# The order of wide and narrow products in a feed-forward layer: alternating, or in runs of one width

## The chip, the core and the metric

The kernel runs on one core of a Trainium2 chip. The metric is the device time of one execution in microseconds, the median of several. TensorE (PE in the profile) multiplies, VectorE (DVE) and ScalarE (ACT) do the elementwise work, GpSimd (POOL) a few small things, and SyncE (SP) issues the loads of the weights.

## What is computed

A decoder trunk of four layers over 256 tokens of width 1024, in float32. Each layer normalises its input, mixes tokens (differential attention, block-sparse attention, sliding-window attention, and differential attention again), adds the result to the residual stream, and then does the same with a feed-forward block; a last normalisation follows. The change is in the feed-forward block alone:

```python
def sqrelu_mlp(h, w_up, w_down):          # w_up 1024 x 4096, w_down 4096 x 1024
    a = jnp.maximum(h @ w_up, 0)
    return (a * a) @ w_down

for i in range(DEPTH):
    ...
    h = h + y                             # y: the token mixer
    h = h + sqrelu_mlp(rms_norm(h, mlp_norm_g[i]), mlp_w_up[i], mlp_w_down[i])
return rms_norm(h, final_norm_g)
```

## The kernel before

Float32 products are made out of products of a faster type, fp32r. Each operand x is split into a high part, x rounded to fp32r, and a low part, the rest. A product is then high times high, plus high times low, plus low times high. Weights arrive in 185 pieces of 128 x 2048 numbers (class `Piece`): SP loads a piece into `raw`, ACT writes the high part `whi`, DVE writes the low part `wlo`, each in two halves of 1024 columns. Four `raw` and three `whi`/`wlo` buffers go round. The activations are kept the same way: for the up projection in `n.both` (tiles hg0 to hg3, `n.lo` is the task that finishes the low part), for the down projection in the tiles uu, listed in `us`. In both, the high and the low part of a block of 128 rows lie side by side, 256 tokens each, so that one matmul can stream both: 512 columns.

That is what `block_step` uses. With a block of 128 x 128 weights stationary, its first matmul streams high and low activations past the high weights, 512 columns, into the whole of a PSUM bank; its second streams the high activations past the low weights, 256 columns, into the first half of the same bank. Eight such steps make a block of 128 rows of the up projection, 32 a block of the down projection. The two halves of the bank are added afterwards (`joined`, tiles cross and relu).

- `up_proj`: 16 groups g of one piece each; a group makes two blocks b of 128 rows (two banks of one PSUM pair, `p_up`), each summed over 8 blocks k of the input. In group 0 the list is sorted by k, since the inputs arrive one after another.
- `down_proj` (layers 0 to 2): 8 blocks d of the output in `p_down`, two pieces h each, 16 steps k per piece.
- `down_out` (layer 3): here the activations are stationary and the weights stream, so that the output comes out with tokens on partitions. There are two halves c of 512 output columns, for each 8 pieces q with 4 steps k, and two token blocks t. Each step is three matmuls (`mm3`) into `p_last`. In the second half, token block 1 is computed as two blocks of 256 columns, and in the last piece one of them is finished before the other. Behind it stand `ended` (DVE adds the residual into `res`, ACT squares it for the norm, DVE multiplies by the gain into `last`) and `send` (a mean on DVE, a power on POOL, and the scaling and the output transfers on ACT with its queue and on DVE with SP's).

The order of all instructions is set by a planner (class `Plan`) at build time: each task has a cost in microseconds and the tasks that it waits for, the planner simulates the engines with those costs, and the instructions are issued in the order of its start times. Main products (`product`) are chained: each waits for the one written before it, so their order among themselves is that of the code. The costs given to `product` decide only what the planner believes of the time. Nothing of the costs is executed. Every instruction has line 191 of the helper class `Ordered` in the profile, so groups are told apart by tile names.

Of the kernel before, what the change touches and what calls it, by code (L numbers as in the profile page):

```python
# [18 lines left out]
P = 128  # L19
D = 1024  # L20
S = 256
NT = S // P
# [175 lines left out]
def trunk(ctx: ExitStack, tc: tile.TileContext, xT, gains, lams, swa_row, fng, weights, out):  # L198
# [8 lines left out]
    def bank(name, i=0):  # L207
        j = plan.now.got["wk"][i] if plan.now else 0
        return ps.tile([P, 512], F32, tag=f"wk{j}", name=name, bufs=1)
# [8 lines left out]
    def r3(n):  # L218
        return lambda t: t.rearrange("p (a b) -> p a b", a=n)
# [23 lines left out]
    def pe(cost, do, after=(), rank=1, **kw):  # L243
        return add("PE", cost, do, after, lag=0.3, rank=rank, **kw)
# [3 lines left out]
    def product(cost, do, after, take=None):  # L248

        main[0] = t = pe(cost, do, [*after, main[0]], 2, take=take)  # L250
        main[1] += cost
        t.done = main[1]
        return t

    def matmul(o, lhsT, rhs, start, stop):
        T.matmul(o, lhsT, rhs, start=start, stop=stop, skip_group_check=True)
# [4 lines left out]
    def mm3(o, lh, ll, rh, rl, start, stop):  # L261
        matmul(o, lh, rh, start, False)
        matmul(o, lh, rl, False, False)
        matmul(o, ll, rh, False, stop)
# [47 lines left out]
    def piece(**kw):  # L312
        pieces.append(Piece(len(pieces), **kw))
        return pieces[-1]

    def release(x):
        give("w", [main[0]], x.hi[0])
# [222 lines left out]


    PRODUCTS = ((0, 0), (1, 0), (0, 1))

    def proj(n, width, **kw):

# [3 lines left out]
        for x in range(count):  # L549
            w = piece(**kw)  # L550
            ks = range(per * x, per * x + per)
            steps = [(t, k, a, b) for k in ks for a, b in PRODUCTS for t in range(NT)]
            for at, (t, k, a, b) in enumerate(steps):
# [431 lines left out]

    def block_step(p, hi, lo, x, start, stop):
        matmul(r3(2)(p), hi, x, start, False)
        matmul(p[:, :S], lo, x[:, 0], False, stop)  # L990

    def joined(o, p, after):

# [41 lines left out]
    def up_proj(n, then):  # L1035

        us = []
        for g in range(16):
            w = piece()
            st = {}  # L1040
            order = [(b, k) for b in range(2) for k in range(8)]
            if g == 0:
                order.sort(key=lambda x: x[1])
            for at, (b, k) in enumerate(order):

                def do(b=b, k=k, w=w, st=st):
                    if not st:
                        st["p"] = two_banks("p_up")
                    c = slice(P * b, P * b + P)
                    block_step(st["p"][:, b], w.at(0, 8, k)[:, c], w.at(1, 8, k)[:, c], n.both[k // 2][:, k % 2],  # L1050
                               k == 0, k == 7)

                t = product(0.347, do, [n.lo[k], w.ready(1, 8, k)], {"acc": 1} if at == 0 else None)
                begin = t if at == 0 else begin
            release(w)

            def sum_to(st=st):
                st["t"] = sb.tile([P, 512], F32, tag="relu", name="relu")
                return r3(2)(st["t"])

            a = joined(sum_to, lambda st=st: st["p"], [t])
            give("acc", [a], begin)

            def squared(st=st):
                st["u"] = sb.tile([P, 512], F32, tag="u", name="u")
                V.scalar_tensor_tensor(st["u"], st["t"], 0.0, st["t"], op0=OP.max, op1=OP.mult)

            def high(st=st, g=g):
                st["both"] = room(g, [P, 2, 2, S], "uu", F32R)
                A.activation(st["both"][:, :, 0], r3(2)(st["u"]), AF.Copy)  # L1070

            def low(st=st):
                V.tensor_tensor(st["both"][:, :, 1], r3(2)(st["u"]), f(st["both"][:, :, 0]), op=OP.subtract)

            a = dve(512, squared, [a])
            a = act(512, high, [a])
            a = dve(512, low, [a])
            us += [(a, lambda st=st, b=b: st["both"][:, b]) for b in range(2)]
            then(g)
        return us  # L1080

    def down_proj(us, n, row):

        def into(j, p, last, begin):

            st = {}

            def to():
                st["y"] = sb.tile([P, 512], F32, tag="y", name="y")
                return r3(2)(st["y"])  # L1090

            def scaled():
                V.tensor_tensor(r3(2)(st["y"]), r3(2)(st["y"]), row[0][:, None, :].to_broadcast([P, 2, S]), op=OP.mult)
                V.tensor_tensor(hT[j], st["y"], hT[j], op=OP.add)

            a = joined(to, p, [last])
            s = dve(1024, scaled, [a, row[1]], 2)
            n.part(2 * j, [s])
            n.part(2 * j + 1, [s])
            n.sum(j, [s])  # L1100
            give("acc", [a], begin)

        for d in range(8):
            if d % 2 == 0:
                st = {}
            for h in range(2):
                w = piece()
                for k in range(16):

                    def do(d=d, h=h, k=k, w=w, st=st):  # L1110
                        if not st:
                            st["p"] = two_banks("p_down")
                        block_step(st["p"][:, d % 2], w.at(0, 16, k), w.at(1, 16, k), us[16 * h + k][1](),
                                   h + k == 0, h == 1 and k == 15)

                    t = product(0.347, do, [us[16 * h + k][0], w.ready(1, 16, k)],
                                {"acc": 1} if d % 2 + h + k == 0 else None)
                    begin = t if d % 2 + h + k == 0 else begin
                release(w)
            if d % 2:  # L1120
                into(d // 2, lambda st=st: st["p"], t, begin)

    def down_out(us, res, factor):

        st = {}
        ss = cst.tile([P, NT, 4], F32, name="fss")
        x = cst.tile([P, NT], F32, name="fx")
# [49 lines left out]
        for c in range(2):  # L1177
            banks, ends = {}, []
            for q in range(8):
                w = piece()  # L1180
                steps = [(t, k, 0, 512) for k in range(4) for t in range(NT)]
                if q == 7 and c:
                    steps = [(0, k, 0, 512) for k in range(4)] + [(1, k, x, x + S) for x in (0, S) for k in range(4)]
                for at, (t, k, lo, hi) in enumerate(steps):

                    def do(t=t, k=k, lo=lo, hi=hi, w=w, q=q, c=c, banks=banks):
                        if not banks:
                            if c:
                                banks.update({x: bank("p_last", i) for i, x in enumerate(((0, 0), (1, 0), (1, 1)))})
                            else:  # L1190
                                both = two_banks("p_last")
                                banks.update({(t, x): both[:, t, S * x:] for t in range(NT) for x in range(2)})
                        u, s = us[4 * q + k][1](), slice(P * t, P * t + P)
                        o = banks[t, 0][:, lo:hi]
                        if c and t:
                            for x in range(lo // S, hi // S):
                                mm3(banks[t, x][:, :S], u[:, 0, s], u[:, 1, s], w.at(0, 4, k)[:, S * x:S * x + S],
                                    w.at(1, 4, k)[:, S * x:S * x + S], q + k == 0, q + k == 10)
                        else:
                            mm3(o, u[:, 0, s], u[:, 1, s], w.at(0, 4, k)[:, lo:hi], w.at(1, 4, k)[:, lo:hi],  # L1200
                                q + k == 0, q + k == 10)

                    z = product(0.68 * (hi - lo) / 512, do, [us[4 * q + k][0], w.ready(1, 4, k)],
                                {("wk" if c else "acc"): 3 if c else 1} if q + at == 0 else None)
                    if q == 7 and k == 3:
                        ends.append((t, lo, hi, z))
                release(w)
            for t, lo, hi, z in ends:
                ended(t, lambda t=t, lo=lo, hi=hi, c=c, banks=banks: banks[t, lo // S][:, :hi - lo],
                      512 * c + lo, 512 * c + hi, 2 * c + (lo > 0), ends[-1][-1] if c == 0 else z)  # L1210
                if c and hi == 512:
                    send(t)


# [3 lines left out]
    n = Normed(gv[:, 0, 0, :])  # L1218

    for i in range(DEPTH):  # L1220
# [10 lines left out]
        n = Normed(gv[:, 1, i, :])  # L1231
# [43 lines left out]
        us = up_proj(n, then)  # L1275
        if i + 1 < DEPTH:
            n = Normed(gv[:, 0, i + 1, :])
# [87 lines left out]
```

## Time and profile before

| | |
|---|---|
| median of 3 runs | 1150.59 us (1150.44 to 1151.76) |
| the profiled execution | 1151.71 us |
| its span, first to last instruction | 1149.9 us |
| PE busy | 1138.5 us, 6558 matmuls |
| DVE, ACT, POOL busy | 814.0, 650.6, 42.6 us |
| an up projection, a down projection of layers 0 to 2 | 90.45, 90.46 us |
| both halves of the last product | from 1054.4 us to about 1142.8 us of the span |

Layers run one after the other: a mixer stage of 77 to 119 us, then the up projection, then the down projection. Durations of matmuls are modelled to their ends and overlap, so their sum is no time of a stage; a stage's time is read from the distance between the starts of its first and last instruction. A row of the timeline gives start, length, engine, operation, output and inputs. A row of waits gives who waited for whom, for how long in all, how often, and the longest.

### The profile page before, as it was taken

Reading aid. Unit: us, or ns where it says so; the run is one execution under the profiler, and the core shown is the slowest. Engines: PE = TensorE matmul, PEld = TensorE weight load, DVE = VectorE, ACT = ScalarE, POOL = GpSimd, SP = SyncE. Lnnn points to the kernel's source line nnn. Section 1 sums busy time; section 2 is a strip of 40 time slices with the busy share of each in tenths; the row PEclk is TensorE's granted clock in tenths of the full one; section 3 lists DMA queues with packets and bytes.
Section 4 is the critical chain, followed back from the end, with each engine's and each line's share of the span. In section 5 each row is a group of like instructions: output and inputs, shape, how many; then the busy total and the mean of one; then the engine's idle time right before and its main releaser. Section 6 shows DMA issues by size and latency. Waiting matters only on the chain.

```text
span 1149.9 us, 16761 instructions
## 1 busy us (share of the span) xinstructions
PE 1138.5 (99%) x6558; PEld 987.7 (86%) x6558; DVE 814.0 (71%) x1385; ACT 650.6 (57%) x1126; POOL 42.6 (4%) x71
## 2 busy tenths in 40 slices
PE   9999999999999999999999999999999999999997
PEld 7889888888888898888887888888888899888886
DVE  8886887656676678765568788765568777877453
ACT  7877655444486655544446765544446776555342
POOL 1000000000100000000011000000010000100000
PEclk9999999999999999999999999999999999999999
DMA  8444555555544455555553165555544445556531
GB/s 305 181 147 151 216 184 183 183 183 184 169 147 160 142 186 187 183 183 184 183 179 138 41 253 184 183 183 183 186 161 168 146 146 185 184 183 201 188 142 37
DMA packets 30031, 198.65 MB, mean 173 GB/s; under 512 B 3456, under 2 KB 4864, under 8 KB 6528
## 3 DMA queue, kind: packets, MB, share of 16 engines
q1 hardware_dynamic: 29664, 197.19, 49.2%
q8 instruction: 51, 0.84, 0.3%
q10 hardware_dynamic: 288, 0.39, 0.1%
q14 instruction: 28, 0.23, 0.1%
HBM read 196.52 MB, written 1.05 MB: 172 GB/s over the span
## 4 chain that ended last, share of the span: by engine, by line
PE 98%; DVE 1%; issue 0%; DMA 0%; POOL 0%; ACT 0%; POOLq 0%; DVEq 0%
PE p_up L191 31%; PE p_down L191 24%; PE p_in L191 20%; PE p_d L191 8%; PE p_last L191 7%; PE p_s L191 3%; PE p_av L191 2%; PE p_t L191 1%; PE p_qk L191 1%; PE p_o L191 0%; DVE qn L191 0%; DVE turns L191 0%; PE p_res L191 0%; DMA gn<-in_gains 0%; DVE an L191 0%
## 5 line engine op out<-in xcount | busy, mean ns | idle before, releaser
L191 DVE TENSOR_TENSOR wlo<-raw,whi 128x1024 fp32r<-128x1024 f32 (+1 forms) x374 | 441.6, 1213 | 220.1 <-ACT whi L191 219.3
L191 ACT ACTIVATE whi<-raw 128x1024 fp32r<-128x1024 f32 (+1 forms) x374 | 374.3, 1043 | 328.3 <-issue 112.5
L191 PE MATMUL p_up<-hg,whi 128*128 128x512 f32 x1024 | 362.2, 399 | 0.0
L191 PE MATMUL p_up<-hg,wlo 128*128 128x256 f32 x1024 | 287.6, 281 | 0.0
L191 PE MATMUL p_down<-uu,whi 128*128 128x512 f32 x768 | 271.5, 399 | 0.0
L191 PEld LDWEIGHTS p_up<-hg,whi 128*128 128x128 f32 x1024 | 192.4, 188 | 47.8
L191 PE MATMUL p_down<-uu,wlo 128*128 128x256 f32 x768 | 215.7, 281 | 0.0
L191 PEld LDWEIGHTS p_up<-hg,wlo 128*128 128x128 f32 x1024 | 193.5, 189 | 0.0
L191 PE MATMUL p_in<-whi,hg 128*128 128x512 f32 (+1 forms) x672 | 187.1, 391 | 0.8 <-DVE hg L191 0.8
L191 PEld LDWEIGHTS p_down<-uu,whi 128*128 128x128 f32 x768 | 144.3, 188 | 36.1
L191 PEld LDWEIGHTS p_down<-uu,wlo 128*128 128x128 f32 x768 | 145.1, 189 | 0.0
L191 PEld LDWEIGHTS p_in<-whi,hg 128*128 128x128 f32 x672 | 122.1, 188 | 24.2 <-DVE hg L191 1.2
L191 PE MATMUL p_in<-wlo,hg 128*128 128x512 f32 (+1 forms) x336 | 105.8, 390 | 0.4 <-DVE wlo L191 0.4
L191 PE MATMUL p_d<-oo,whi 128*128 128x256 f32 x512 | 96.7, 289 | 0.0
L191 PE MATMUL p_last<-whi,uu 128*128 128x256 f32 (+1 forms) x320 | 82.2, 347 | 0.0
L191 PEld LDWEIGHTS p_d<-oo,whi 128*128 128x128 f32 x512 | 80.2, 193 | 1.3 <-issue 1.1
L191 PEld LDWEIGHTS p_in<-wlo,hg 128*128 128x128 f32 x336 | 62.0, 188 | 12.9 <-DVE wlo L191 0.8
L191 PE MATMUL p_d<-oo,wlo 128*128 128x256 f32 x256 | 72.9, 285 | 0.0
L191 ACT ACTIVATE e<-ns,nm 128x128 f32<-128x128 f32 (+3 forms) x128 | 57.1, 449 | 15.8 <-DVE nm L191 15.1
L191 PEld LDWEIGHTS p_last<-whi,uu 128*128 128x128 f32 x320 | 55.8, 188 | 7.9
L191 ACT ACTIVATE uu<-u 128x512 fp32r<-128x512 f32 x64 | 39.9, 624 | 33.2 <-DVE u L191 33.2
L191 PE MATMUL p_last<-wlo,uu 128*128 128x256 f32 (+1 forms) x160 | 55.6, 347 | 0.0
(155 smaller groups left out, 1002.6 us busy)
## 6 DMA issues: line engine op xcount, KB each, us to landing
raw<-in_weights SPq DMA_DIRECT2D x183, 1024.0 KB, 4.9
raw<-in_weights SPq DMA_DIRECT2D x8, 256.0 KB, 5.2
hT<-in_xT SPq DMA_DIRECT2D x8, 128.0 KB, 4.9
out<-last SPq DMA_DIRECT2D x2, 320.0 KB, 2.4
bias<-in_swa_row SPq DMA_DIRECT2D x1, 512.0 KB, 3.9
grow<-in_fng SPq DMA_DIRECT2D x1, 512.0 KB, 5.1
out<-last ACTq DMA_DIRECT2D x2, 192.0 KB, 2.3
lv<-in_lams SPq DMA_DIRECT2D x1, 256.0 KB, 7.8
```

The lines of the kernel that those rows point to most:

```text
L191: x = getattr(self.engine, name)(*args, **kw)
```

## The change

`block_step` issues one of its two matmuls, chosen by `part`. The loops of `up_proj` and `down_proj` go over the parts outside the steps k: for each block of the up projection all eight 512-column matmuls, then all eight 256-column ones; for each piece of the down projection sixteen of the one kind and then sixteen of the other. Group 0 of the up projection is still sorted by k, and so still alternates. Each matmul is now a task of its own, with a cost from `STEPS`, and waits for its own part of the weights (`w.ready(part, ...)`) where the pair waited for the low part. In `down_out` the second half's token block 1 is computed in 512 columns like block 0; its two 256-column halves are still finished and scaled by separate instructions, now both behind the last product.

```diff
+    STEPS = (0.2267, 0.12)
...
-    def block_step(p, hi, lo, x, start, stop):
-        matmul(r3(2)(p), hi, x, start, False)
-        matmul(p[:, :S], lo, x[:, 0], False, stop)
+    def block_step(p, w, x, part, start, stop):
+        if part:
+            matmul(p[:, :S], w, x[:, 0], False, stop)
+        else:
+            matmul(r3(2)(p), w, x, start, False)
...
-            order = [(b, k) for b in range(2) for k in range(8)]
+            order = [(b, part, k) for b in range(2) for part in range(2) for k in range(8)]
             if g == 0:
-                order.sort(key=lambda x: x[1])
+                order.sort(key=lambda x: x[2])
...
-                t = product(0.347, do, [n.lo[k], w.ready(1, 8, k)], {"acc": 1} if at == 0 else None)
+                t = product(STEPS[part], do, [n.lo[k], w.ready(part, 8, k)], {"acc": 1} if at == 0 else None)
...
-                for k in range(16):
+                for part, k in ((part, k) for part in range(2) for k in range(16)):
...
-                steps = [(t, k, 0, 512) for k in range(4) for t in range(NT)]
+                steps = [(t, k) for k in range(4) for t in range(NT)]
                 if q == 7 and c:
-                    steps = [(0, k, 0, 512) for k in range(4)] + [(1, k, x, x + S) for x in (0, S) for k in range(4)]
+                    steps.sort()
...
-            for t, lo, hi, z in ends:
-                ended(t, lambda t=t, lo=lo, hi=hi, c=c, banks=banks: banks[t, lo // S][:, :hi - lo],
-                      512 * c + lo, 512 * c + hi, 2 * c + (lo > 0), ends[-1][-1] if c == 0 else z)
-                if c and hi == 512:
+            for t, z in ends:
+                for lo, hi in ((0, 512),) if c == 0 or t == 0 else ((0, S), (S, 512)):
+                    ended(t, lambda t=t, lo=lo, hi=hi, banks=banks: banks[t][:, lo:hi],
+                          512 * c + lo, 512 * c + hi, 2 * c + (lo > 0), ends[-1][-1] if c == 0 else z)
+                if c:
                     send(t)
```

Two places show what moves. The first is PE in layer 0's up projection, group 1 (piece 17, first block; hg0 to hg3 are the activations, and each hg tile holds two of the eight steps). Before:

```order
L191 MATMUL p_up_1494<-hg0_1415,whi17_1375 128x512
L191 MATMUL p_up_1494<-hg0_1415,wlo17_1376 128x256
...
L191 MATMUL p_up_1494<-hg1_1425,whi17_1375 128x512
L191 MATMUL p_up_1494<-hg1_1425,wlo17_1376 128x256
...
L191 MATMUL p_up_1494<-hg2_1455,whi17_1375 128x512
```

After:

```order
L191 MATMUL p_up_1494<-hg0_1415,whi17_1375 128x512 x2
L191 MATMUL p_up_1494<-hg1_1425,whi17_1375 128x512 x2
L191 MATMUL p_up_1494<-hg2_1454,whi17_1375 128x512 x2
L191 MATMUL p_up_1494<-hg3_1463,whi17_1375 128x512 x2
L191 MATMUL p_up_1494<-hg0_1415,wlo17_1376 128x256 x2
L191 MATMUL p_up_1494<-hg1_1425,wlo17_1376 128x256 x2
L191 MATMUL p_up_1494<-hg2_1454,wlo17_1376 128x256 x2
L191 MATMUL p_up_1494<-hg3_1463,wlo17_1376 128x256 x2
```

The eight low products have moved behind the eight high ones. The down projection moves alike, sixteen behind sixteen.

The second is the end of the program on DVE: the finishing of the last token blocks, res0 and last0 for block 0, res1 and last1 for block 1, fss the sums of squares, fx and fr the norm's factor. Before:

```order
L191 SCALAR_TENSOR_TENSOR res0_9266<-p_last_10327,factor_152,res0_9266 128x512
L191 TENSOR_TENSOR last0_9471<-res0_9266,grow_9473 128x512
L191 SCALAR_TENSOR_TENSOR res1_9267<-p_last_10328,factor_152,res1_9267 128x256
L191 TENSOR_REDUCE fx_155<-fss_154 128x1
L191 TENSOR_SCALAR fx_155<-fx_155 128x1
L191 TENSOR_TENSOR last1_9472<-res1_9267,grow_9473 128x256
L191 SCALAR_TENSOR_TENSOR res1_9267<-p_last_10329,factor_152,res1_9267 128x256
...
L191 TENSOR_SCALAR last0_9471<-last0_9471,fr_156 128x640
```

After:

```order
L191 SCALAR_TENSOR_TENSOR res0_9265<-p_last_10327,factor_152,res0_9265 128x512
L191 TENSOR_TENSOR last0_9469<-res0_9265,grow_9471 128x512
L191 TENSOR_REDUCE fx_155<-fss_154 128x1
L191 TENSOR_SCALAR fx_155<-fx_155 128x1
L191 SCALAR_TENSOR_TENSOR res1_9266<-p_last_10328,factor_152,res1_9266 128x256 x2
L191 TENSOR_TENSOR last1_9470<-res1_9266,grow_9471 128x256 x2
L191 TENSOR_SCALAR last0_9469<-last0_9469,fr_156 128x640
```

Both halves of block 1 now stand behind block 0's mean, in one row, and both come from one bank (p_last_10328).

More of the change, by code (lines that the diff above doesn't have):

```diff
@@ L1040, in up_proj, with do @@
             st = {}
-            order = [(b, k) for b in range(2) for k in range(8)]
+            order = [(b, part, k) for b in range(2) for part in range(2) for k in range(8)]
             if g == 0:
-                order.sort(key=lambda x: x[1])
-            for at, (b, k) in enumerate(order):
-                def do(b=b, k=k, w=w, st=st):
+                order.sort(key=lambda x: x[2])
+            for at, (b, part, k) in enumerate(order):
+                def do(b=b, part=part, k=k, w=w, st=st):
                     if not st:
                         st["p"] = two_banks("p_up")
-                    c = slice(P * b, P * b + P)
-                    block_step(st["p"][:, b], w.at(0, 8, k)[:, c], w.at(1, 8, k)[:, c], n.both[k // 2][:, k % 2],
+                    block_step(st["p"][:, b], w.at(part, 8, k)[:, P * b:P * b + P], n.both[k // 2][:, k % 2], part,
                                k == 0, k == 7)
-                t = product(0.347, do, [n.lo[k], w.ready(1, 8, k)], {"acc": 1} if at == 0 else None)
+                t = product(STEPS[part], do, [n.lo[k], w.ready(part, 8, k)], {"acc": 1} if at == 0 else None)
                 begin = t if at == 0 else begin
@@ L1107, in down_proj, with do @@
                 w = piece()
-                for k in range(16):
-                    def do(d=d, h=h, k=k, w=w, st=st):
+                for part, k in ((part, k) for part in range(2) for k in range(16)):
+                    def do(d=d, h=h, k=k, part=part, w=w, st=st):
                         if not st:
                             st["p"] = two_banks("p_down")
-                        block_step(st["p"][:, d % 2], w.at(0, 16, k), w.at(1, 16, k), us[16 * h + k][1](),
+                        block_step(st["p"][:, d % 2], w.at(part, 16, k), us[16 * h + k][1](), part,
                                    h + k == 0, h == 1 and k == 15)
-                    t = product(0.347, do, [us[16 * h + k][0], w.ready(1, 16, k)],
-                                {"acc": 1} if d % 2 + h + k == 0 else None)
-                    begin = t if d % 2 + h + k == 0 else begin
+                    at = d % 2 + h + k + part
+                    t = product(STEPS[part], do, [us[16 * h + k][0], w.ready(part, 16, k)], {"acc": 1} if at == 0 else None)
+                    begin = t if at == 0 else begin
                 release(w)
@@ L1180, in down_out @@
                 w = piece()
-                steps = [(t, k, 0, 512) for k in range(4) for t in range(NT)]
+                steps = [(t, k) for k in range(4) for t in range(NT)]
                 if q == 7 and c:
-                    steps = [(0, k, 0, 512) for k in range(4)] + [(1, k, x, x + S) for x in (0, S) for k in range(4)]
-                for at, (t, k, lo, hi) in enumerate(steps):
-                    def do(t=t, k=k, lo=lo, hi=hi, w=w, q=q, c=c, banks=banks):
+                    steps.sort()
@@ L1187, in do @@
+                for at, (t, k) in enumerate(steps):
+                    def do(t=t, k=k, w=w, q=q, c=c, banks=banks):
                         if not banks:
                             if c:
-                                banks.update({x: bank("p_last", i) for i, x in enumerate(((0, 0), (1, 0), (1, 1)))})
+                                banks.update({x: bank("p_last", x) for x in range(NT)})
                             else:
                                 both = two_banks("p_last")
-                                banks.update({(t, x): both[:, t, S * x:] for t in range(NT) for x in range(2)})
+                                banks.update({x: both[:, x] for x in range(NT)})
@@ L1193, in do @@
                         u, s = us[4 * q + k][1](), slice(P * t, P * t + P)
[L1194 to L1201, printed above, removed]
@@ L1203, in down_out @@
-                    z = product(0.68 * (hi - lo) / 512, do, [us[4 * q + k][0], w.ready(1, 4, k)],
-                                {("wk" if c else "acc"): 3 if c else 1} if q + at == 0 else None)
+                        mm3(banks[t], u[:, 0, s], u[:, 1, s], w.at(0, 4, k), w.at(1, 4, k), q + k == 0, q + k == 10)
+                    z = product(0.68, do, [us[4 * q + k][0], w.ready(1, 4, k)],
+                                {("wk" if c else "acc"): 2 if c else 1} if q + at == 0 else None)
                     if q == 7 and k == 3:
-                        ends.append((t, lo, hi, z))
+                        ends.append((t, z))
```

## The prediction

> **What bounds the kernel now.** I read the page first: the busy times, then the chain that ended last.
>
> ```profile
> span 1149.9 us, 16761 instructions
> PE 1138.5 (99%) x6558; PEld 987.7 (86%) x6558; DVE 814.0 (71%) x1385; ACT 650.6 (57%) x1126; POOL 42.6 (4%) x71
> PE 98%; DVE 1%; issue 0%; DMA 0%; POOL 0%; ACT 0%; POOLq 0%; DVEq 0%
> ```
>
> TensorE is 98% of the chain, so time is won or lost by how closely matmuls follow each other. The waits view of PE alone says whether it starves:
>
> ```profile
> PE p_qk L191 <- DVE oo L191: 2.2, 1, 2.2
> PE p_warm L191 <- DVE minus_half L191: 1.1, 1, 1.1
> PE p_in L191 <- DVE hg L191: 0.8, 1, 0.8
> PE p_in L191 <- DVE wlo L191: 0.4, 1, 0.4
> ```
>
> 4.5 us in all, none of it in the feed-forward products. The changed stages, from the chain in order of time (start, length, what), with the p_in stage behind them; the other layers show the same 90.45 and 90.46, layer 3's p_up with a few transposes among it:
>
> ```profile
> 119.24 90.45 PE p_up L191 x512
> 209.69 90.46 PE p_down L191 x512
> 300.16 15.20 PE p_in L191 x67
> ```
>
> Matmul durations (281 and 399 ns) are not what one costs, since each starts before the last ends. The price is the distance between starts, a window divided by its matmuls. p_up and p_down alternate 512 and 256 columns: 90.45/256 = 353.3 ns a pair, in both stages. What do the widths cost among their own kind? I cut windows that begin and end on the start of a matmul: the first two hold nothing but 256-column p_d products (layers 3 and 0), the third nothing but 512-column p_last products of the first half, the fourth 26 repetitions of three 512-column and six 256-column products (second half). In each, x counts one or two matmuls still running at the window's start. The columns are the stretch, its length, PE's busy time and count, granted clock, DMA share and GB/s.
>
> ```profile
> 948.56:960.80 12.24, 12.24 (x104) 1.00 0.48 174
> 110.62:119.24 8.62, 8.62 (x73) 1.00 0.57 212
> ```
> ```profile
> 1061.33:1098.05 36.72, 36.72 (x163) 1.00 0.55 183
> 1100.03:1136.60 36.57, 36.57 (x236) 1.00 0.17 59
> ```
>
> So 102 of 256 columns take 120.0 ns each (72 in the other stretch 119.7), 162 of 512 take 226.7; a pair ought to take 346.7 ns and takes 353.3. The fourth row is the proof that width changes are what costs: 36.57/26 = 1406.5 ns, against 3 x 226.7 + 6 x 120.0 = 1400.0. One change from 512 to 256 and back costs 6.5 ns there, 6.65 ns in p_up, whether the runs are 3 and 6 long or 1 and 1. The rows of PE in p_up show where it sits: 0.24 from a 512's start to the 256 behind it (226.7 in a run), 0.12 from the 256 to the next 512.
>
> ```profile
> 150.17 0.40 PE L191 MATMUL p_up<-hg,whi 128*128 128x512 f32 x1
> 150.41 0.28 PE L191 MATMUL p_up<-hg,wlo 128*128 128x256 f32 x1
> 150.53 0.40 PE L191 MATMUL p_up<-hg,whi 128*128 128x512 f32 x1
> 150.77 0.28 PE L191 MATMUL p_up<-hg,wlo 128*128 128x256 f32 x1
> ```
>
> **The change part by part.** *Runs in p_up and p_down.* The trace has no 512-column run with the weights stationary, as p_up will have it. Its pitch lies between 226.7 (the weights moving) and 353.3 - 120.0 = 233.3 ns, what such a product takes now ahead of a narrow one; below 226.7 nothing points, since p_in and p_last, with different operands, share that pitch to 0.2 ns (15.20 us for 67 in the chain). I take 226.7, because the fourth row finds the excess at the change of width also with the other operand form. The matmuls are the same; what goes is width changes. Per layer p_up has 256 pairs, so 256 changes (512 to 256 and back). After it, the first group still alternates (16) and the other 15 have two each: 46. Four layers: 840 gone. p_down has 256 in each of three layers; after, one per piece, 16: 720 gone. 1560 x 6.65 ns = 10.4 us. It all lies on the path, since PE waits for nothing there. A p_up stage should take 90.45 - 210 x 0.00665 = 89.05 us, a p_down stage 90.46 - 240 x 0.00665 = 88.86.
>
> *Columns of the last product.* In its second half, token block 1 goes from six matmuls of 256 to three of 512 in each of 32 steps. Before: 28 steps at 1.4065, then 4 x 3 x 0.2267 and 8 x 3 x 0.12: 39.38 + 2.72 + 2.88 = 44.98 us. After: 192 x 0.2267 = 43.52. Gain 1.5 us.
>
> *The tail.* Here the last block loses its cover: half of it used to be finished, scaled and squared while the other half was computed. The rows of DVE, ACT and PE at the end:
>
> ```profile
> 1142.69 0.28 PE L191 MATMUL p_last<-whi,uu 128*128 128x256 f32 x1
> ```
> ```profile
> 1141.58 0.48 DVE L191 SCALAR_TENSOR_TENSOR res<-p_last,factor,res 128x256 f32<-128x256 f32 x1
> 1141.98 0.14 DVE L191 TENSOR_REDUCE fx<-fss 128x1 f32<-128x4 f32 x1
> 1142.23 0.42 DVE L191 TENSOR_TENSOR last<-res,grow 128x256 f32<-128x256 f32 x1
> 1143.01 0.48 DVE L191 SCALAR_TENSOR_TENSOR res<-p_last,factor,res 128x256 f32<-128x256 f32 x1 [0.37 <-PE p_last L191]
> 1143.53 0.42 DVE L191 TENSOR_TENSOR last<-res,grow 128x256 f32<-128x256 f32 x1
> 1143.87 0.55 DVE L191 TENSOR_SCALAR last<-last,fr 128x640 f32<-128x640 f32 x1
> 1144.70 0.16 DVE L191 TENSOR_REDUCE fx<-fss 128x1 f32<-128x4 f32 x1 [0.28 <-ACT sq L191]
> ```
> ```profile
> 1142.09 0.42 ACT L191 ACTIVATE sq<-res 128x256 f32<-128x256 f32 x1 [0.44 <-DVE res L191]
> 1142.42 0.19 ACT L191 ACTIVATION_READ_ACCUMULATOR sq<-res 128x1 f32 x1
> 1143.73 0.38 ACTq L191 DMA_DIRECT2D out<-last  x1
> 1144.16 0.42 ACT L191 ACTIVATE sq<-res 128x256 f32<-128x256 f32 x1 [0.45 <-DVE last L191]
> ```
>
> Let E be the last matmul's start plus its own pitch: 1142.69 + 0.12 = 1142.81. The span ends 7.1 us after E, and its last link off PE is the reduce at E + 1.89; what follows it is unchanged. After the change DVE issues res, res, last, last, then the scaling of block 0 ahead of that reduce. From E + 0.20 (1143.01) that is 0.48 + 0.48 + 0.42 + 0.42 + 0.55 = 2.35 us, less some 0.07 at each joint (1143.53 to 1143.87 is 0.34 for an operation of 0.42): the reduce comes at E + 2.2 to E + 2.55. ACT has both squares (0.52 each, 1142.09 to 1142.61) behind block 0's scaling and the issue of its output DMA, which ended at 1144.11, E + 1.30; block 0 now finishes 2.72 us ahead of E, not 2.88, but its reduce no longer stands behind a res, so about E + 1.1 + 1.04 = E + 2.15. Late next, then, is DVE. Cost 0.3 to 0.65 us, taken 0.5; the ends are 0, if ACT's lead and DVE's overlap are larger than these rows, and 1.3 (0.48 + 0.42 + 0.42, all work of the half in series).
>
> *What loses cover.* PE asks for things earlier. In p_down the sixteen 512-column products come first, so the second half of whi is needed after 8 x 0.2267 = 1.8 us of a piece and not 2.8; wlo is needed later. Splits are done well ahead: a piece's wlo is finished at 202.43 and the next one's at 208.08, while PE begins those pieces at 209.69 and, 16 pairs on, at 215.3.
>
> ```profile
> 200.07 2.36 DVE L191 TENSOR_TENSOR wlo<-raw,whi 128x1024 fp32r<-128x1024 f32 x2 [0.26 <-ACT whi L191]
> 205.72 2.36 DVE L191 TENSOR_TENSOR wlo<-raw,whi 128x1024 fp32r<-128x1024 f32 x2 [0.26 <-ACT whi L191]
> 212.89 0.68 DVE L191 TENSOR_TENSOR uu<-u,uu 128x512 fp32r<-128x512 f32 x1
> ```
>
> The last uu is ready at 213.57 and needed 30 pairs into p_down, at 220.3; after, 16 x 0.3467 + 14 x 0.2267 = 8.7 us in: 4.8 us of cover left. DVE and ACT are moved a little among themselves in p_up, with the same operations. SP's queue is moved at one place: layer 2's two bias loads now stand behind one more weight load.
>
> ```profile
> 588.66 0.33 SPq L940 DMA_DIRECT2D bias<-in_swa_row x1
> 589.37 0.33 SPq L941 DMA_DIRECT2D rest<-in_swa_row x1
> 591.37 36.73 SPq L290 DMA_DIRECT2D raw<-in_weights x5
> ```
> ```profile
> rest<-in_swa_row SPq DMA_DIRECT2D x1, 136.0 KB, 4.9
> ```
> ```profile
> 601.28 0.16 DVE L191 TENSOR_SCALAR rest<-rest 128x16 f32<-128x16 f32 x1
> ```
>
> That load went out at 591.37, so the second bias load goes out some 2.7 us later, near 592.4; it needed 4.9 us to land (the second fence, of the page's DMA issues), and its first reader ran at 601.28: 4 us of cover. I cost all this at nothing; were the cover gone, each piece would wait for its split, DVE's 2.4 us, and layer 2 for its bias, a microsecond or two.
>
> *The clock.* One stretch ran below full clock, layer 2's mixer, where PE was idle for the 2.2 us of the first waits row:
>
> ```profile
> 593.58:670.96 77.38, 75.08 (x484) 64.16 (x483) 61.57 (x168) 53.72 (x133) 8.53 (x17) 0.98 0.34 120
> ```
>
> A mean of 0.98 over 77.4 us is about 1.5 us lost. The change does not touch that stretch, so I cost it at nothing, but another execution may pay it or not: 1.5 us either way. [...]
>
> *Sum:* -10.4 - 1.5 + 0.5 = -11.4 us. The profiled execution took 1151.71 us, 1.8 beyond its span and 1.1 above the median of the runs, 1150.59 (1150.44 to 1151.76). From the profiled one it gives 1140.3, from the median 1139.2; the measured time is a median too, so 1139.3.
>
> **The rivals.** *The price is each product's own.* If the 6.65 ns belong to the 512-column product as p_up makes it (weights stationary, both halves of a moving pair), whatever stands beside it, runs change nothing: -1.5 + 0.5, 1149.6 us. For it: the run that the trace lacks. Against: the 6.5 ns of the fourth window row, with weights as the moving operand. [...]
>
> *Long narrow runs fall behind their weight loads (slower).* A weight load lasts longer than a 256-column pitch:
>
> ```profile
> L191 PEld LDWEIGHTS p_up<-hg,wlo 128*128 128x128 f32 x1024 | 193.5, 189 | 0.0
> ```
>
> Now a wide product stands before each narrow one and may hide its load. If 8 to 16 narrow ones in a row fell to 189 ns, 1728 x 69 ns would be 119 us more, 1258. It decides from 120 + 11.4/1.728 = 126.6 ns up. Against: p_d's 102 narrow products, each with a load of its own, keep 120.0.
>
> *Finer waits give part of it back.* The moved products outrun uu or a freed PSUM pair now and then; half of the gain lost, 1145. Against: the cover of 4.8 us and more above.
>
> **How the numbers follow.** Less than 0.2% is about what a measurement of this kernel cannot tell from no change, 2.3 us. Forecast 0.88, price of the product 0.05, waits 0.04, narrow runs 0.03. Faster takes the first and third, 0.92; same 0.05; slower 0.03. The likeliest case has its ends from the terms: 6.4 to 6.9 ns a change by the other pitches quoted (10.0 to 10.8 us), the tail 0 to 1.3, the clock 1.5 either way. All at once on one side they give 1136.8 and 1142.0; 0.8 more above for a first part of the third rival. 1136.8 to 1142.8 leaves out the other rivals and a few hundredths of the forecast, and is the range.
>
> **What would show it.** Right: p_up 89.0 us and p_down 88.9 in the chain, uniformly, with 227 ns and 120 ns between starts inside runs; the second half of p_last at 43.5; the last reduce 2.2 to 2.6 us after E. Wrong: stages still at 90.4 (the first rival), narrow runs above 126 ns (the second), PE waits named p_up or p_down (the third), or a mixer stage several us longer.

## The result, and the profile after

The changed kernel took 1142.7 us, the median of 4 runs (1140.85 to 1143.92), against 1150.97 us (1150.44 to 1151.76, 4 runs) for the kernel before beside it. The ratio is 0.9926, 95% interval 0.9909 to 0.9943: 8.3 us gained where 11.4 were forecast. The time lies 0.1 us inside the upper end of the range.

The profiled execution took 1142.88 us. From its page:

```profile
span 1141.1 us, 16569 instructions
PE 1128.6 (99%) x6462; PEld 983.4 (86%) x6462; DVE 814.4 (71%) x1385; ACT 650.1 (57%) x1126; POOL 42.3 (4%) x71
PE 98%; DVE 1%; issue 0%; DMA 0%; ACT 0%; POOLq 0%; POOL 0%; DVEq 0%
```

The 96 matmuls that are gone are those of the last product (32 steps with three for six). TensorE is the bound as before. PE's waits, the whole list:

```profile
PE p_qk L191 <- DVE oo L191: 2.2, 1, 2.2
PE p_in L191 <- DVE hg L191: 1.4, 1, 1.4
PE p_warm L191 <- DVE minus_half L191: 1.1, 1, 1.1
PE p_in L191 <- DVE wlo L191: 0.4, 1, 0.4
PE p_in L191 <- ACT whi L191: 0.3, 1, 0.3
```

None of them names p_up, p_down or p_last. The stages, from the chain in order of time (start, length):

```profile
119.71 89.47 PE p_up L191 x512
209.18 89.07 PE p_down L191 x512
298.25 15.22 PE p_in L191 x67
...
410.79 89.47 PE p_up L191 x512
500.27 89.07 PE p_down L191 x512
```

An up projection went from 90.45 to 89.47 us (forecast 89.05), a down projection from 90.46 to 89.07 (forecast 88.86). Both moved the right way and fell short, by 0.42 and 0.21 us. The third layer's pair shows the same two numbers.

Where the difference lies shows inside a down projection. Three windows of the changed kernel's trace follow one piece: from the start of its first wide product to that of its sixth, from there to the first narrow one, and from there to the next piece's first wide one (stretch, length, PE busy and count, clock, DMA share, GB/s; the count includes one or two matmuls still running at the start):

```profile
231.28:232.44 1.16, 1.16 (x7) 1.00 1.00 423
232.44:234.94 2.49, 2.49 (x12) 1.00 0.17 30
234.94:236.85 1.91, 1.91 (x17) 1.00 0.85 253
```

Five products in 1.16 us are 232 ns each; eleven in 2.49 us are 226, the plain pitch within the rounding; sixteen narrow ones in 1.91 us are 119 to 120. So after a narrow run the first five wide products are slow, by 1.16 - 5 x 0.2267 = 0.027 us together, and a little comes back in the narrow run (1.91 against 16 x 0.12 = 1.92). The whole piece, 231.28 to 236.85, takes 5.57 us against 16 x 0.34667 = 5.547: about 20 ns for one change of width and back. The alternation paid 6.65 ns for each of its many changes.

The tail, where E is the last matmul's start plus its pitch (the distance from one start to the next), 1133.56 + 0.23 = 1133.79:

```profile
1133.56 0.39 PE L191 MATMUL p_last<-whi,uu 128*128 128x512 f32 x1
```
```profile
1133.98 0.88 DVE L191 SCALAR_TENSOR_TENSOR res<-p_last,factor,res 128x256 f32<-128x256 f32 x2 [0.83 <-PE p_last L191]
1134.78 0.75 DVE L191 TENSOR_TENSOR last<-res,grow 128x256 f32<-128x256 f32 x2
1135.44 0.55 DVE L191 TENSOR_SCALAR last<-last,fr 128x640 f32<-128x640 f32 x1
1135.91 0.15 DVE L191 TENSOR_REDUCE fx<-fss 128x1 f32<-128x4 f32 x1
```

The reduce comes at E + 2.12, where it was at E + 1.89; the span ends 7.3 us after E, not 7.1. The tail costs 0.2 us.

The account of the two spans, 1149.9 and 1141.1: the first mixer +0.47 (119.24 to 119.71; in the ten profiles of this case it ends anywhere between 118.88 and 120.70), up projections -0.98 three times and -1.0 in layer 3, down projections -1.39 three times, the other mixers +0.1, the last product -1.46, the tail +0.2. Together -8.8, which is the difference.

### The profile page after: what moved, and what is told of

It reads as the page before. It is cut to its first block, busy times and chain, and to the rows that moved or that the text cites. A ratio compares the mean times of both kernels' runs of the same rounds, so it can differ in the third digit from the quotient of the medians.

```text
span 1141.1 us, 16569 instructions
## 1 busy us (share of the span) xinstructions
PE 1128.6 (99%) x6462; PEld 983.4 (86%) x6462; DVE 814.4 (71%) x1385; ACT 650.1 (57%) x1126; POOL 42.3 (4%) x71
## 4 chain that ended last, share of the span: by engine, by line
PE 98%; DVE 1%; issue 0%; DMA 0%; ACT 0%; POOLq 0%; POOL 0%; DVEq 0%
PE p_up L191 31%; PE p_down L191 23%; PE p_in L191 20%; PE p_d L191 8%; PE p_last L191 7%; PE p_s L191 3%; PE p_av L191 2%; PE p_t L191 1%; PE p_qk L191 1%; PE p_o L191 0%; DVE qn L191 0%; DMA gn<-in_gains 0%; DVE turns L191 0%; PE p_res L191 0%; DVE an L191 0%
## 5 line engine op out<-in xcount | busy, mean ns | idle before, releaser
L191 PE MATMUL p_up<-hg,whi 128*128 128x512 f32 x1024 | 263.2, 393 | 0.0
L191 PEld LDWEIGHTS p_up<-hg,whi 128*128 128x128 f32 x1024 | 184.7, 189 | 33.8
L191 PE MATMUL p_down<-uu,whi 128*128 128x512 f32 x768 | 183.2, 391 | 0.0
L191 PE MATMUL p_up<-hg,wlo 128*128 128x256 f32 x1024 | 151.9, 282 | 0.0
L191 PEld LDWEIGHTS p_up<-hg,wlo 128*128 128x128 f32 x1024 | 143.1, 190 | 9.4
L191 PEld LDWEIGHTS p_down<-uu,wlo 128*128 128x128 f32 x768 | 98.5, 191 | 3.7
L191 PE MATMUL p_down<-uu,wlo 128*128 128x256 f32 x768 | 99.6, 283 | 0.0
L191 PE MATMUL p_last<-whi,uu 128*128 128x512 f32 x256 | 78.9, 389 | 0.0
L191 PEld LDWEIGHTS p_last<-whi,uu 128*128 128x128 f32 x256 | 48.1, 188 | 9.9
L191 DVE TENSOR_TENSOR relu<-p_up,cross 128x512 f32<-128x512 f32 x64 | 43.9, 686 | 10.7 <-ACT cross L191 10.7
```

What stands on the lines that cost most here:

```text
L191: x = getattr(self.engine, name)(*args, **kw)
```

## The experiments

The theory that the trace after suggests: a change from narrow to wide slows the next five wide products by a fixed sequence, so what a change costs depends on how long the wide run behind it is, and the gain is set by changes of width alone. The rivals: the excess belongs to the wide product itself, to the start of a piece or PSUM bank, or to the planner's new order on DVE and ACT. Each edit is shown against the changed kernel, but for the last.

**The same kernel again**, as a reference beside the next three.

> The changed kernel once more, on the chip of the three runs sent with it. Its profile had p_up at 89.47 us and p_down at 89.07, against 90.45 and 90.46 before, and the last 1.7 us gained in p_last and its tail. If the width changes are what moved, those stage times return to 0.05 us. What differs from run to run (1140.85 to 1143.92) I expect outside the feed-forward stages, where the granted clock dips. Median 1141 to 1144, ratio 0.991 to 0.994.

Median 1142.51 us (1142.4 to 1143.74, 5 runs), ratio 0.9925, interval 0.9912 to 0.9937. The stages repeat to the last digit:

```profile
119.58 89.47 PE p_up L191 x512
209.05 89.07 PE p_down L191 x512
```

**The runs alone**, with the last product as before:

```diff
-                steps = [(t, k) for k in range(4) for t in range(NT)]
+                steps = [(t, k, 0, 512) for k in range(4) for t in range(NT)]
                 if q == 7 and c:
-                    steps.sort()
+                    steps = [(0, k, 0, 512) for k in range(4)] + [(1, k, x, x + S) for x in (0, S) for k in range(4)]
...
```

> The runs alone; the last product as before, in 256 columns for token block 1. Theory (the gain is in the number of width changes): p_up 89.47 and p_down 89.07 us as in the changed kernel, so 4 x 0.98 + 3 x 1.39 = 8.1 us less than before: ratio 0.993. Rival (the planner's new order of DVE and ACT, or the last product, brought it): stages back near 90.4, ratio near 1.

1143.44 us (1143.37 to 1144.89, 5 runs), ratio 0.9935, interval 0.9922 to 0.9947.

```profile
119.87 89.47 PE p_up L191 x512
209.35 89.07 PE p_down L191 x512
...
1047.07 85.68 PE p_last L191 x456
```

**The last product alone**, with the old `block_step` and the old loops:

```diff
-    def block_step(p, w, x, part, start, stop):
-        if part:
-            matmul(p[:, :S], w, x[:, 0], False, stop)
-        else:
-            matmul(r3(2)(p), w, x, start, False)
+    def block_step(p, hi, lo, x, start, stop):
+        matmul(r3(2)(p), hi, x, start, False)
+        matmul(p[:, :S], lo, x[:, 0], False, stop)
...
```

> The last product in 512 columns alone; the feed-forward products alternate as before. Theory: the second half of p_last takes 43.5 us instead of 45.0 and the tail 0.2 us more, so 1.2 us less than before: ratio 0.999, hard to tell from no change by time, but to be read in the profile. p_up and p_down at 90.45 and 90.46.

1150.23 us (1148.86 to 1153.08, 11 runs), ratio 0.9989, interval 0.998 to 0.9997.

```profile
120.70 90.45 PE p_up L191 x512
211.15 90.46 PE p_down L191 x512
...
1057.08 84.36 PE p_last L191 x372
```

The two parts, 0.9935 and 0.9989, multiply to 0.9924: they account for the whole, and the stages move with the part that touches them and not with the other. A hidden effect of the planner is not needed.

**Fewer changes.** The up projection does both blocks' wide products, then both blocks' narrow ones; of two pieces of the down projection the second is mirrored, so the wide run of one block meets that of the next. The flags that open and close a sum in PSUM move with the first and the last product.

```diff
-            order = [(b, part, k) for b in range(2) for part in range(2) for k in range(8)]
+            order = [(b, part, k) for part in range(2) for b in range(2) for k in range(8)]
...
-                for part, k in ((part, k) for part in range(2) for k in range(16)):
+                for part, k in ((part, k) for part in (range(2) if h == 0 else (1, 0)) for k in range(16)):
```

> Half as many width changes as the changed kernel: up projection 16 wide then 16 narrow products per group (both blocks), down projection wide, narrow, narrow, wide over two pieces. Theory T (a switch from narrow to wide slows the five wide products behind it by 27 ns in all, and the first narrow ones give 7 back: 20 ns per change in long runs): p_up 89.47 to 89.12 us, p_down 89.07 to 88.91, 1.9 us in all, ratio to before 0.991. Rival A (every wide product of this form costs 1 to 2 ns more, whatever its place): 89.47 and 89.07 stay. Rival B (the start of a piece or of a PSUM bank is what costs 20 ns): p_up stays at 89.47, as it still begins two banks per group, and p_down at 89.07. Rival C (6.65 ns per change, as forecast): 0.1 us less in each stage.

1140.46 us (1140.37 to 1140.92, 4 runs), ratio 0.9904, interval 0.9889 to 0.992.

```profile
119.72 89.07 PE p_up L191 x512
208.80 88.93 PE p_down L191 x512
```

Theory: 89.12 and 88.91. All three rivals had p_up at 89.37 or above and miss it: the products, pieces and banks are the same in number, only the changes are fewer. That also settles the starts of pieces and banks: there are as many of them as before, and the second block of each group now starts its bank amid a wide run. In the up projection 15 long changes are gone, and group 0 goes two wide, two narrow where it alternated. Group 0, from its first start to that of group 1, in the changed kernel and here:

```profile
119.54:125.19 5.65, 5.65 (x34) 1.00 0.11 14
119.56:125.13 5.57, 5.57 (x34) 1.00 0.09 13
```

Its sixteen pairs would take 5.547 us without a change. So group 0 gives 0.08 us of the 0.40, and a long change is worth 0.32/15 = 21 ns; in the down projection (89.07 - 88.93)/8 = 17 ns. The eight changes that group 0 keeps cost (5.57 - 5.547)/8, about 3 ns each: less than in strict alternation.

**Runs of four.**

```diff
-            order = [(b, part, k) for b in range(2) for part in range(2) for k in range(8)]
+            order = [(b, part, k) for b in range(2) for k4 in (0, 4) for part in range(2) for k in range(k4, k4 + 4)]
...
-                for part, k in ((part, k) for part in range(2) for k in range(16)):
+                for part, k in ((part, k) for k4 in (0, 4, 8, 12) for part in range(2) for k in range(k4, k4 + 4)):
```

> Runs of four wide and four narrow products in up and down projection (group 0 of the up projection alternates as in the changed kernel). The base, without any change of width, is 256 x 346.67 = 88.75 us a stage. Theory T (what a change costs is spent over the first five wide products behind it, as the changed kernel's pitches show: 6.8, 9.2, 1.8, 5.4, 4.2 ns, less 7.5 given back in the narrow run; a run of four ends it early): about 15.8 ns a change, 60 changes in an up projection and 64 in a down projection: p_up 89.80, p_down 89.76 us. Rival (a fixed 20 ns per change): 90.07 and 90.05. Rival C (6.65 ns per change, as forecast): 89.25 and 89.18.

1146.12 us, one run.

```profile
119.25 89.85 PE p_up L191 x512
209.10 89.81 PE p_down L191 x512
```

89.85 and 89.81, 0.05 above the theory and 0.2 below the fixed 20 ns. A change costs (89.81 - 88.75)/64 = 16.6 ns in runs of four. So the price per change depends on the run, and does not simply grow with it: 6.65 ns in runs of one, about 3 in runs of two (group 0 above), 16.6 in runs of four, about 20 in runs of eight and sixteen, (89.07 - 88.75)/16. Per pair that is 6.65, 1.5, 4.1, 2.5 and 1.25. The theory's sequence, cut short, fits from four on; for runs of two it would give 6.8 + 9.2 - 7.5 = 8.5 ns, so in short runs the sequence is not fixed. Why is open.

**All wide.** The low-weight product streams 512 columns as well, and so adds the product of the two low parts.

```diff
-        if part:
-            matmul(p[:, :S], w, x[:, 0], False, stop)
-        else:
-            matmul(r3(2)(p), w, x, start, False)
+        matmul(r3(2)(p), w, x, start and not part, stop and part == 1)
```

> The order of the changed kernel, but the low-weight product streams all 512 columns too (it adds the product of the two low parts, which the other kernels leave out). No change of width is left in up and down projection, while pieces, PSUM banks and the order of weights begin where they did. Theory T (only the change of width costs): 512 x 226.67 ns = 116.05 us a stage, pitch 227 ns from the first product on. Rival A (wide products with stationary weights cost 1 to 2 ns more in themselves): 116.6 to 117.1. Rival B (20 ns at the start of each block or piece): p_up 116.65, p_down 116.37.

1329.49 us, one run.

```profile
118.88 116.08 PE p_up L191 x512
234.96 116.05 PE p_down L191 x512
```

116.05 is 512 x 226.67 ns. With the weights stationary and no change of width, the pitch is the plain one to 0.1 ns, over all the starts of pieces, banks and weight tiles: rivals A and B give 116.4 and more. The up projection has 0.03 us on top: its first wide products stand behind the narrow ones of p_d, and five behind a narrow run lost 0.027 us in the changed kernel.

**448 columns** instead of 256 for the low-weight product.

```diff
-            matmul(p[:, :S], w, x[:, 0], False, stop)
+            matmul(p[:, :448], w, x.rearrange("p a b -> p (a b)")[:, :448], False, stop)
```

> The order of the changed kernel, with the low-weight product at 448 columns instead of 256 (it adds a part of the product of the low parts). By the two known pitches one such product takes 120 + 192 x 106.7/256 = 200 ns, so the base is 256 x 426.7 = 109.23 us a stage. What sets the size of the slow stretch behind a change? T1 (the step in columns, here a quarter): about 5 ns a change, p_up 109.4, p_down 109.3 us. T0 (any change of width): 20 ns a change, 109.9 and 109.6. T2 (only products shorter than the 188 ns that a weight load lasts set it off): no slow stretch, 109.23 in both.

1291.61 us, one run.

```profile
119.92 110.80 PE p_up L191 x512
230.72 110.19 PE p_down L191 x512
```

All three numbers were missed, because the base was wrong: a run of 448-column products does not go at 200 ns. A timeline of PE in the down projection shows three runs:

```profile
271.88 3.81 PE L191 MATMUL p_down<-uu,whi 128*128 128x512 f32 x16
275.53 3.40 PE L191 MATMUL p_down<-uu,wlo 128*128 128x448 f32 x16
278.77 3.81 PE L191 MATMUL p_down<-uu,whi 128*128 128x512 f32 x16
```

Sixteen 448s from 275.53 to 278.77 are 202.5 ns each. Is that their own pitch, or a slow start as in the wide run? Windows that begin and end on a start tell: five wide products and the five behind them, then three times five 448s in a row.

```profile
271.88:273.04 1.15, 1.15 (x7) 1.00 0.04 14
273.04:274.17 1.13, 1.13 (x7) 1.00 0.00 0
275.53:276.54 1.01, 1.01 (x7) 1.00 0.67 153
276.54:277.56 1.01, 1.01 (x7) 1.00 1.03 404
277.56:278.57 1.01, 1.01 (x7) 1.00 0.93 396
```

The 448s do not settle: each five take 1.01 us, from 275.53 to 278.57 fifteen take 3.04, so 202.7 ns is the pitch of 448 columns by themselves. The wide run does settle, as behind a 256-column run: its first five are slow by about 0.02 us (0.027 in the changed kernel), the next five are plain. With the base put right, 256 x (226.7 + 202.7) = 109.9 us, a change costs (110.19 - 109.9)/16, about 17 ns, and in the up projection (110.80 - 109.9)/46, about 20 ns on average, the alternating group 0 included. That is near the 20 ns of T0, with a quarter of the step in columns and with products whose pitch of 202.7 ns is longer than a weight load, 188 ns on the page of the kernel before: T1 and T2 are out.

**Mirrored groups.** As the order with fewer changes, against which the edit is shown, and every second group of the up projection begins with its narrow products.

```diff
+            turn = (1, 0) if g % 2 else (0, 1)
-            order = [(b, part, k) for part in range(2) for b in range(2) for k in range(8)]
+            order = [(b, part, k) for part in turn for b in range(2) for k in range(8)]
...
```

> The order with half as many changes, and every second group of the up projection mirrored as well (narrow products first, then wide), so that wide runs meet wide runs and narrow runs narrow ones: 8 long changes in an up projection instead of 15. Theory T: p_up 89.07 to 88.93 us, p_down 88.93 as it was, 0.6 us in all: about 1140 us, ratio to before 0.990. If starting a bank with the narrow product costs something, p_up stays at 89.07 or rises.

1138.8 us (1137.79 to 1140.12, 4 runs), ratio 0.9879, interval 0.9862 to 0.9895.

```profile
119.55 88.94 PE p_up L191 x512
208.49 88.91 PE p_down L191 x512
```

88.94, as the theory has it, 0.2 us above a stage without any change. This is the best version: 0.53 us less per up and 0.16 less per down projection than the changed kernel, 2.6 us by the profile. The profiled executions of the two, both with a mean granted clock of 0.997, are as far apart: 1142.70 us for the same kernel again and 1140.12 for this one. The medians, 1142.51 and 1138.8, are 1.1 us further apart; two of the four runs here had a clock of 0.999, and none of the five there.

## Why the prediction was right, and which term was not

- *The mechanism was right.* The price is in changes of width, not in the products: the kernels with fewer changes, with none, and with mirrored groups show it from three sides, and the first rival, the price of the product, falls with 116.05 us for 512 wide products in a row of the very form that the trace before lacked.
- *The mis-sized term is "1560 x 6.65 ns = 10.4 us".* It measured 8.1 us (4 x 0.98 + 3 x 1.39). The count of changes was right; the step that failed is the sentence that one change costs 6.5 ns "whether the runs are 3 and 6 long or 1 and 1", carried over to runs of 8 and 16. There the changes that remain cost 20 ns each and not 6.65: 30 in an up projection, (89.47 - 88.75 - 0.11 for the alternating group 0)/30 = 20 ns, and 16 in a down projection, (89.07 - 88.75)/16 = 20 ns. The two cases that agreed, runs of 3 and 6 and runs of 1 and 1, were both short, and their agreement was taken for a constant; runs of two (3 ns) and of four (16.6) show that it was a coincidence. The bounds quoted, 6.4 to 6.9 ns, measured how well the pitches are known, and not how the price could depend on length. The prediction had named 226.7 to 233.3 ns for the wide product and taken the lower end: the sixteen of a run take 1.16 + 2.49 = 3.65 us, 228 each. The trace before held a warning. In the first mixer, wide p_in products stand behind eight 128-column transposes; from the second of them on, five take 1.16 us, and the next five 1.13:

```profile
33.36:34.52 1.16, 1.16 (x6) 1.00 0.56 234
34.52:35.66 1.13, 1.13 (x7) 1.00 0.03 7
```

- *The columns of the last product* gave 1.46 us where 1.5 was forecast; alone, they make a ratio of 0.9989.
- *The tail* cost 0.2 us, not 0.5, and less than the 0.3 to 0.65 that the rows gave. DVE's four operations took 0.88 + 0.75 in pairs, less than the 0.48 + 0.48 + 0.42 + 0.42 of single file, and the reduce waited for neither engine long: E + 2.12 against a forecast of E + 2.2 to 2.55.
- *What lost cover cost nothing*, as forecast: no wait of PE names the changed stages, with DVE's and ACT's order moved in p_up. Of layer 2's two bias loads, the second went out 1.3 us ahead of the mixer's start and not 4.2, and still landed ahead of its reader:

```profile
588.06 0.55 SPq L942 DMA_DIRECT2D rest<-in_swa_row  x1
```

  With 5.8 us to landing, 593.9; the reader ran at 597.0. The cover was 3.1 us, not 4.
- *The narrow runs* keep 119 to 120 ns over sixteen products, each with a load of its own that lasts 190 ns in p_up and 191 in p_down, by the profile after: the slower rival is out.
- *That the time still lies in the range is luck.* The term missed by 2.3 us where it had been given 0.4. The room came from terms that do not explain the miss: 0.8 us for the tail, 1.5 for the clock and 0.8 for a rival. Without the clock's, the range would have ended at 1141.3; that an execution may pay those 1.5 us or not was the author's estimate from one trace. Layer 2's mixer took 77.26 to 77.44 us in nine profiles and 78.57 in the tenth; the two mirrored runs at a clock of 0.999, 1137.79 and 1138.52 us against 1140.12 in the profiled one, have no profile. The tail came cheaper than forecast, the third rival's waits did not come, and that mixer took 77.38 us in the profile before and 77.41 in the one after. By the spans the gain is 8.8 us where 11.4 were forecast. Of the 2.6 that are missing, 2.3 are the price of a change and 0.6 the mixers; the tail gives 0.3 back.

## What to carry to other kernels

Where matmuls of two widths must alternate, try them in long runs, and turn every second block round so that like meets like: here an up projection took 90.45 us alternating, 89.47 in runs and 88.94 with mirrored groups. Do not take it that a longer run is always better: here runs of four cost 4.1 ns per pair and runs of two 1.5. Before carrying a price per event from one arrangement to another, look at the spacing of single products behind the event: here the slow stretch lasts five products (0.027 us), and runs of eight and sixteen pay it in full, about 20 ns a change. The price of matmuls that overlap is read from the distance between starts over a window that begins and ends on a start: here a 512-column one lasts 399 ns in the profile before and costs 226.7.

## What the runs showed of the hardware

- In long runs a 512-column fp32r product has a pitch of 226.7 ns with the weights moving (162 of p_last in 36.72 us, before) as with the weights stationary (116.05 us for 512, all wide), and a 256-column one 120.0 with the weights stationary (102 of p_d in 12.24 us, before) as with the weights moving (22 of p_last from 1140.05 to 1142.69 us, before). Plain float32 is dearer where this case has it: in layer 0's mixer six products with 128 columns (p_av, twelve matmuls in the trace) take 1.25 us, from 51.62 to 52.87 in the profile before, 208 ns each. A 448-column fp32r product has 202.7 ns by itself, more than the 200.0 on the line between the two; that such a width does not lie on the line was not expected. Why the first wide products behind a change are slow, and why runs of two pay so little, stays open: the slow stretch needs no narrow product below a weight load's length (it follows the 448s, 202.7 ns against 188, with 0.02 us), and no new piece and no new bank (in runs of four, 48 of a down projection's 64 changes lie inside a piece and its bank, and a change costs 16.6 ns).
- The granted clock differs from run to run of one kernel and goes with most of their spread: of the eleven runs with the last product alone, the five with a mean granted clock of 0.998 or 0.999 took 1148.86 to 1149.56 us, and the six with 0.995 to 0.997 took 1150.23 to 1153.08. Apart from the two ends of the span, the profiles before and after have one dip to half the clock each, 3.41 us long, in layer 2's mixer: before from 634.41 (first row), 1.37 us behind the end of the 2.2 us wait there, and after from 628.69, 0.12 us ahead of that end. In the profile of the last product alone the dip in this mixer is 6.83 us long (second row), twice as much, and one more of 3.41 us lies near the start (third row). The columns are the stretch, its length, the busy time of PE, PEld, DVE, ACT and POOL, the clock, the DMA share and GB/s:

```profile
634.41:637.83 3.41, 3.41 (x19) 3.41 (x18) 1.90 (x3) 2.61 (x5) 0.00 (x0) 0.50 0.00 0
633.65:640.48 6.83, 5.98 (x28) 6.01 (x29) 4.17 (x11) 3.81 (x8) 0.19 (x1) 0.50 0.00 0
9.01:12.43 3.41, 3.41 (x9) 2.65 (x10) 3.41 (x11) 3.06 (x7) 0.00 (x0) 0.50 1.04 363
```

  The mixer then takes 78.57 us at a mean of 0.96, where the profile before has 77.38 at 0.98:

```profile
595.04:673.61 78.57, 76.27 (x483) 65.37 (x483) 61.64 (x168) 53.81 (x133) 8.54 (x17) 0.96 0.34 118
```

  In the other eight the mixer takes 77.26 to 77.44 us, and all ten have the 2.2 us wait. So the place of the dip repeats in the three profiles above, 38.6 to 40.8 us into the mixer, and its length does not; what sets the length, or a further dip, was not shown.
